# A hybrid decoder trunk on one core: matmuls of a stage grouped by width, attention distances seeded into the score banks by ScalarE, compress sums on 64 stationary columns

## The chip, the cores and the metric

The kernel runs on one core of a Trainium2 chip. The metric is the device time of one execution in microseconds. The core has TensorE (matmuls, with a weight load before each), VectorE, ScalarE, GpSimd and SyncE, which issues the DMAs; each takes its own queue of instructions in order.

## What is computed

Two layers over 256 tokens of 2048 features, in fp32. Each layer projects the normalized input with one matrix (2048 x 5696), whose columns feed three groups of heads; their outputs go through `w_out`, then an MLP of width 8192, then a gated per-layer embedding.

```python
def hybrid_layer(h, p_i, ...):
    proj = rms_norm(h, norm_mix_pre) @ w_in
    o_a = nsa_mixer(nsa_q, nsa_kv, nsa_g, nsa_cmp_w, nsa_cmp_pe)   # 16 heads in 4 groups, 64 wide
    o_b = rglru_mixer(...)
    o_c = gla_mixer(...)
    h = h + rms_norm(concatenate([o_a, o_b, o_c]) @ w_out, norm_mix_post)
    u = rms_norm(h, norm_mlp_pre)
    h = h + rms_norm(jnp.square(jax.nn.relu(u @ w_up)) @ w_down, norm_mlp_post)
    return h + jax.nn.sigmoid(h @ w_ple_gate) * (p_i @ w_ple)

def nsa_mixer(...):                       # three branches per head
    # compressed: 15 windows of 32 tokens, each summed with a learned weight to one key and one value
    k_cmp, v_cmp = compress(kc, cmp_w[0], cmp_pe[0]), compress(vc, cmp_w[1], cmp_pe[1])
    s = q @ k_cmp - slope * d_cmp         # then a softmax over valid windows, times v_cmp
    # selected blocks and sliding window, both with their own keys and values:
    s = q @ k - slope * distance          # causal softmax, times v
    return g0 * o_cmp + g1 * o_sel + g2 * o_win
```

With 256 tokens there are four blocks to select from and 16 may be selected, so all causal keys take part in the second branch, and the window of 512 covers everything too.

## The kernel before

Weights stream from HBM in units of 128 x 1024 elements. `ensure` takes a unit from a list in a fixed order (`plan`): SyncE loads it into `raw`, ScalarE casts it to `hi` (a shortened fp32 that TensorE takes at full rate), and VectorE makes the remainder `lo`. There are eight `hi` and eight `lo` buffers, so ScalarE and VectorE work up to eight units ahead, and a cast waits until TensorE has read the old content of its buffer. A product of two numbers is then three: hi x hi, hi x lo and lo x hi.

Two kinds of stage use the units. `form_a` keeps the activations stationary and moves 512 (or 256, 320) weight columns, three matmuls for each 128 rows of the weights. `form_b` keeps 128 columns of weights stationary and moves the activations: one matmul of 512 columns for `hi` (the activations' hi and lo side by side) and one of 256 columns for `lo`. It goes through the unit bank by bank: for each of `nf` banks of PSUM, for each of `kpu` blocks of rows, first the 512-column matmul, then the 256-column one. In the wide form (MLP) `nf` is 4 and `kpu` 2, in the narrow form (projections) 2 and 4, so a unit has eight pairs either way. A wide stage has eight units (64 pairs), a narrow one four (32 pairs); a layer has 15 wide and 16 narrow ones.

Attention and the recurrences are Python generators in a background list. After each unit `pump` runs pieces of them, each up to its next `yield`, so that their instructions stand among the projections; the number that a `yield` gives is an estimated time in us. Dependencies and the final order on each engine are worked out by the scheduler of the tile framework, which may move an instruction ahead of its place in the program when its inputs and buffers are ready.

`compress` (L705) builds blocks of the key and value inputs on VectorE and sums them with full-fp32 matmuls, each of which the profile shows as two instructions. The key sums keep 64 weight columns stationary and move 32; the value sums keep 128 block columns stationary and move 64 weight columns. Keys and values are done in one piece each, with one `yield` between them. `nsa` (L756) then has one piece for the scores of compressed keys, and for each of 8 pairs of heads three score tiles `S` of 512 columns. Each begins with a matmul of `idr` (an identity) with `dr` (the distances), which writes the distances into the bank (L804, L811); the products of queries with keys are added by the matmuls behind it. VectorE takes the maximum, ScalarE the exponentials straight from the bank, TensorE transposes and multiplies with the values, on 64 stationary columns in each half of the bank. `S` uses two banks (`sc`) in turn.

Of the kernel before, what the change touches and what calls it, by code (L numbers as in the profile page):

```python
# [18 lines left out]
P = 128  # L19
# [17 lines left out]
RATE = 1.02  # L37

C_D, C_DC, C_SL, C_SLC, C_RV, C_GM, C_SM = 0, 256, 288, 352, 384, 386, 514
C_ID = C_END = 770  # L40


def consts():
    c = np.zeros((P, C_END + P), np.float32)
    p = np.arange(P)
    slope = np.exp2(np.float32(-8.0) * np.arange(1, NH + 1, dtype=np.float32) / np.float32(NH)).astype(np.float32)
    c[:, C_ID:C_ID + P] = np.eye(P)
    c[:, C_D:C_D + 128] = p[None, :] - p[:, None] - 128
    c[:, C_D + 128:C_D + 256] = np.where(p[None, :] <= p[:, None], p[None, :] - p[:, None], NEG)
    for hf in range(2):  # L50
        t = p + 128 * hf
        d = t[:, None] - (16 * np.arange(15)[None, :] + 31)
        c[:, C_DC + 16 * hf:C_DC + 16 * hf + 15] = np.where(d >= 0, -d, NEG)
        c[:, C_DC + 16 * hf + 15] = 2 * NEG
        c[:, C_RV + hf] = (t >= 31)
    for cc in range(2):
        for f in range(4):
            for hf in range(2):
                for x in range(2):
                    sl = slope[8 * cc + 2 * f + x]  # L60
                    c[:, C_SL + (cc * 4 + f) * 8 + hf * 4 + x * 2:C_SL + (cc * 4 + f) * 8 + hf * 4 + x * 2 + 2] = sl
                    c[:, C_SLC + cc * 16 + hf * 8 + f * 2 + x] = sl
    c[:, C_GM:C_GM + P] = (p[:, None] <= p[None, :]) & (p[:, None] // 64 == p[None, :] // 64)
    c[:, C_SM:C_SM + 256] = (np.arange(256) % 64 != 0)[None, :]
    return c, slope
# [33 lines left out]
class Trunk:  # L99
# [66 lines left out]
    def cst(self):  # L166
        nc = self.nc
        self.c = self.sb.tile([P, C_END], F32, name="cst")
        self.id_ = self.sb.tile([P, P], F32, name="ident")
        self.dma(self.id_, self.a["cst"][:, C_ID:C_ID + P])  # L170
        self.ident = self.id_
        self.mhalf = self.sb.tile([P, 8], F32, name="mhalf")
        nc.gpsimd.memset(self.mhalf, -0.5)

    def cst2(self):
        nc, c = self.nc, self.c
        self.dma(c, self.a["cst"][:, 0:C_END])
        self.idr = self.sb.tile([P, P], F32R, name="idr")
        nc.vector.tensor_copy(self.idr, self.ident)
        self.dr = self.sb.tile([P, 288], F32R, name="dr")  # L180
        nc.vector.tensor_copy(self.dr, c[:, C_D:C_D + 288])


    def ensure(self, i):
# [74 lines left out]
    def form_b(self, base, nu, ut, evac, w=256, which=None, dst=None):  # L259


        nf, kpu = w // 128, 1024 // w
        accs = [self.acc() for _ in range(nf)] if which is None else self.banks(which)
        self.ensure(base)
        for u in range(nu):
            self.ensure(base + u)
            hi, lo = self.loaded[base + u]
            for f in range(nf):
                o = accs[f]
                for k in range(kpu):  # L270
                    kt = kpu * u + k
                    sl = slice(k * w + f * 128, k * w + f * 128 + 128)
                    last = u == nu - 1 and k == kpu - 1
                    self.mm(o, hi[:, sl], ut.both(kt), u == 0 and k == 0, False)
                    self.mm(o[:, 0:T], lo[:, sl], ut.get(kt)[0], False, last)
            self.ensure(base + u + NBUF)
            self.pump(1.4)
        for b in range(nf // 2):
            t = self.t2() if dst is None else dst
            for f in range(2):  # L280
                o, s = accs[2 * b + f], t[:, f * 256:f * 256 + 256]
                self.nc.scalar.copy(s, o[:, T:2 * T])
                self.tt(s, o[:, 0:T], s, ALU.add)
            if evac:
                evac(b, t)
# [419 lines left out]
    def compress(self, kc, wk, cm):  # L705
# [24 lines left out]
        for lp in range(16):  # L730
            for gp in range(2):
                self.mm(b[gp * 64:gp * 64 + 64, 0:32], wkv[0][:, lp], bk[:, lp, gp].rearrange("p c n -> p (c n)"),
                        lp == 0, lp == 15)
        kch = self.st([P, 2, 2, 16], "kch", 1, F32R)
        kcl = self.st([P, 2, 2, 16], "kcl", 1, F32R)
        nc.gpsimd.memset(kcl.bitcast(F32), 0.0)
        for gp in range(2):
            sl, so = slice(gp * 64, gp * 64 + 64), slice(64 - gp * 64, 128 - gp * 64)
            pv = b[sl, 0:32].rearrange("p (c n) -> p c n", c=2)
            nc.scalar.copy(kch[sl, :, gp], pv)  # L740
            nc.vector.tensor_sub(kcl[0:64, :, gp], pv, kch[sl, :, gp].bitcast(F32))
            nc.scalar.copy(kch[so, :, gp], pv)
        yield 0.3
        b = self.tr()
        for lp in range(16):
            self.mm(b[:, 0:64], bv[lp // 8][:, lp % 8].rearrange("p c g n -> p (c g n)"), wkv[1][:, lp], lp == 0, lp == 15)
        vc = self.st([64, 4, 64], "vcmp", 1)
        for g in range(4):
            for x in range(2):
                nc.scalar.copy(vc[x * 32:x * 32 + 32, g], b[g * 32:g * 32 + 32, 0:64])  # L750
        cm["kh"], cm["kl"], cm["v"] = kch, kcl, vc
        if self.dbg:
            self.dbg("vc", [vc, kch, kcl])
        yield 0.8

    def nsa(self, c, qa, kh, kl, v, cm, mhi, mlo):  # L756
        nc = self.nc
        qs = lambda j, hf: qa[j // 4][:, j % 4, hf * 128:hf * 128 + 128]

        S = self.sc()[:, 0:256]  # L760
        for hf in range(2):
            self.mm(S[:, hf * 128:hf * 128 + 128], self.idr,
                    self.dr[:, None, 256 + 16 * hf:272 + 16 * hf].to_broadcast([P, 8, 16]), hf == 0, False)
            for j in range(8):
                o = S[:, hf * 128 + j * 16:hf * 128 + j * 16 + 16]
                self.mm(o, qs(j, hf), cm["kh"][:, c, j // 4], False, False)
                self.mm(o, qs(j, hf), cm["kl"][:, c, j // 4], False, True)
        Sg = S.rearrange("p (x n) -> p x n", n=16)
        mx = self.sm(16)
        nc.vector.tensor_reduce(mx, Sg, axis=AX.X, op=ALU.max, negate=True)  # L770
        pc = self.t2().rearrange("p (x n) -> p x n", n=32)
        nc.gpsimd.memset(pc, 0.0)
        t = self.t2()[:, 0:256].rearrange("p (x n) -> p x n", n=16)
        self.tt(t, Sg, mx[:, :, None].to_broadcast([P, 16, 16]), ALU.add)
        self.tt(t, t, self.c[:, C_SLC + c * 16:C_SLC + c * 16 + 16, None].to_broadcast([P, 16, 16]))
        pcv = pc[:, :, 0:16]
# [6 lines left out]
                self.gtv[:, :, 8 * c:8 * c + 8])  # L783
        self.tt(pcv, pcv, den[:, :, None].to_broadcast([P, 16, 16]))
        pct = self.unit()
        pctv = pct.rearrange("p (j t) -> p j t", j=4)
        for jj in range(2):
            b = self.tr()
# [7 lines left out]
        for j in range(4):  # L796
# [4 lines left out]
            for st in range(3):  # L801
                S = self.sc()
                if st == 0:
                    self.mm(S, self.idr, self.dr[:, None, 128:256].to_broadcast([P, 4, 128]), True, False)  # L804
                    for x in range(2):
                        o = S[:, x * 256:x * 256 + 256]
                        self.mm(o, qs(2 * j + x, 0), kh[c][:, gp, :, 0:128], False, False)
                        self.mm(o, qs(2 * j + x, 0), kl[c][:, gp, :, 0:128], False, True)
                    m0, mw = 0, 4
                else:  # L810
                    self.mm(S, self.idr, self.dr[:, None, 0:256].to_broadcast([P, 2, 256]), True, False)  # L811
                    x = st - 1
                    self.mm(S, qs(2 * j + x, 1), kh[c][:, gp].rearrange("p b k -> p (b k)"), False, False)
                    self.mm(S, qs(2 * j + x, 1), kl[c][:, gp].rearrange("p b k -> p (b k)"), False, True)
                    m0, mw = 4 + 2 * x, 2
                nc.vector.tensor_reduce(mx[:, m0:m0 + mw], S.rearrange("p (x k) -> p x k", x=mw), axis=AX.X, op=ALU.max,
                                        negate=True)
                self.tt(nb[:, m0:m0 + mw], mx[:, m0:m0 + mw], sl8[:, m0:m0 + mw])
                pe = self.t2()
                kk = 512 // mw  # L820
                for x in range(mw):
                    h = 8 * c + 2 * j + (x // 2 if st == 0 else st - 1)
                    self.actf(pe[:, x * kk:x * kk + kk], S[:, x * kk:x * kk + kk], AF.Exp,
                              bias=nb[:, m0 + x:m0 + x + 1], scale=float(self.slope[h]),
                              accum_out=den[:, m0 + x:m0 + x + 1])
                pts.append((pe, m0, mw, kk))
                yield 1.1
# [21 lines left out]
            o = self.tr()[:, 0:T]  # L849
            g = 2 * c + gp  # L850
            for x in range(2):
                self.mm(o[x * 64:x * 64 + 64], cm["v"][x * 32:x * 32 + 16, g], pctv[x * 32:x * 32 + 16, j], True, False)
            for br in range(2):
                for kb in range(2):
                    for x in range(2):
# [247 lines left out]
```

## Time and profile before

| | |
|---|---|
| median of 3 runs | 2561.22 us (2560.81 to 2566.4) |
| the profiled execution | 2562.55 us, span 2560.8 us |
| TensorE busy | 2514.0 us, 98% of the span, 13062 matmuls |
| VectorE, ScalarE, GpSimd busy | 1533.5, 1258.8, 31.0 us |
| mean granted TensorE clock | 0.989 of full speed |

PE is TensorE's matmuls, PEld its weight loads, DVE VectorE, ACT ScalarE, POOL GpSimd. A matmul's row shows out<-moving,stationary. Matmuls overlap, so the mean duration of one is longer than the distance from one start to the next, and the pace of a row of matmuls is read from starts or from whole stretches.

### The profile page before, as it was taken

How to read it: one execution, taken by the hardware profiler on the slowest of the kernel's cores; microseconds unless marked ns; L12 is line 12 of the kernel's file. 1: busy time of each engine (PE TensorE's matmuls, PEld its weight loads, DVE VectorE, ACT ScalarE, POOL GpSimd, SP SyncE). 2: the span in 40 equal slices, each digit the busy share in tenths (PEclk: the TensorE clock that was granted, in tenths of full speed). 3: DMA queues.
4: the chain of work that ended last, by engine and by line, in shares of the span. 5: the costliest groups of instructions: out<-in, count | busy, mean ns of one | idle time of the engine just before them, and what ended most of it. 6: DMA issues, size and time to landing. Idle time of an engine off the chain costs nothing.

```text
span 2560.8 us, 33875 instructions
## 1 busy us (share of the span) xinstructions
PE 2514.0 (98%) x13062; PEld 2115.4 (83%) x13062; DVE 1533.5 (60%) x2088; ACT 1258.8 (49%) x1950; POOL 31.0 (1%) x41
## 2 busy tenths in 40 slices
PE   7999999999999999999999999999999999999999
PEld 7888888788888888887888788887888888888877
DVE  5665667764555555656666656677645556555564
ACT  6564546554443443444455555555544434444452
POOL 1000000000000000000010000000000000000000
PEclk9899999999999999999998999999999999999999
DMA  8543446556655556565564434555566556555653
GB/s 254 163 127 116 137 158 209 156 177 205 189 188 195 186 190 193 186 209 181 181 191 147 124 117 127 175 196 167 187 194 186 191 193 187 191 189 189 206 175 129
DMA packets 286369, 452.15 MB, mean 177 GB/s; under 512 B 32984, under 2 KB 107744, under 8 KB 286208
## 3 DMA queue, kind: packets, MB, share of 16 engines
q1 hardware_dynamic: 286208, 450.00, 55.0%
q8 instruction: 102, 1.67, 0.3%
q14 instruction: 59, 0.48, 0.1%
HBM read 447.85 MB, written 2.10 MB: 176 GB/s over the span
## 4 chain that ended last, share of the span: by engine, by line
PE 92%; DVE 4%; ACT 1%; DMA 1%; issue 1%; POOL 0%; SPq 0%; POOLq 0%; DVEq 0%; ACTq 0%
PE acc L164 61%; PE sc L164 15%; PE tr L164 15%; DVE lo L146 1%; DVE u L149 1%; PE tr L840 1%; PE tr L306 1%; ACT t L161 1%; DVE h L152 0%; DMA raw<-in_w_in_dram 0%; ACT hi L145 0%; DMA t<-in_p_dram 0%; DMA raw<-in_w_up_dram 0%; POOL sm L296 0%; DVE u L152 0%
## 5 line engine op out<-in xcount | busy, mean ns | idle before, releaser
L146 DVE TENSOR_TENSOR lo<-raw,hi 128x1024 fp32r<-128x1024 f32 (+1 forms) x832 | 1008.6, 1213 | 786.5 <-ACT hi L145 783.0
L145 ACT CAST hi<-raw 128x1024 fp32r<-128x1024 f32 (+1 forms) x832 | 867.1, 1044 | 1010.1 <-PE acc L164 586.5
L164 PE MATMUL acc<-hi,u 128*128 128x512 f32 (+2 forms) x2944 | 906.3, 386 | 14.8 <-ACT u L624 10.2
L164 PE MATMUL acc<-u,hi 128*128 128x512 f32 x1920 | 687.6, 401 | 0.0
L164 PEld LDWEIGHTS acc<-hi,u 128*128 128x128 f32 x2944 | 551.6, 190 | 123.1 <-ACT u L624 11.2
L164 PE MATMUL acc<-lo,u 128*128 128x512 f32 (+2 forms) x1472 | 567.4, 386 | 1.2 <-DVE lo L146 1.2
L164 PE MATMUL acc<-u,lo 128*128 128x256 f32 x1920 | 541.7, 282 | 0.0
L164 PEld LDWEIGHTS acc<-u,hi 128*128 128x128 f32 x1920 | 363.4, 189 | 87.8 <-issue 1.3
L164 PEld LDWEIGHTS acc<-u,lo 128*128 128x128 f32 x1920 | 364.9, 190 | 1.2 <-issue 0.3
L164 PEld LDWEIGHTS acc<-lo,u 128*128 128x128 f32 x1472 | 279.6, 190 | 53.2 <-DVE lo L146 1.7
L164 PE MATMUL tr<-u,hi 128*128 128x512 f32 x512 | 186.6, 399 | 0.0
L164 PE MATMUL sc<-u,hi 128*128 128x512 f32 x512 | 186.3, 398 | 0.0
L164 PE MATMUL sc<-u,lo 128*128 128x256 f32 x512 | 143.6, 281 | 0.0
L164 PE MATMUL tr<-u,lo 128*128 128x256 f32 x512 | 143.6, 280 | 0.0
L164 PE MATMUL sc<-hi,u 128*128 128x512 f32 x384 | 119.3, 389 | 0.0
L164 PE MATMUL tr<-hi,u 128*128 128x512 f32 x384 | 119.2, 389 | 0.0
L164 PEld LDWEIGHTS tr<-u,hi 128*128 128x128 f32 x512 | 96.2, 188 | 24.2 <-issue 0.6
L164 PEld LDWEIGHTS sc<-u,hi 128*128 128x128 f32 x512 | 96.2, 188 | 23.6
L164 PEld LDWEIGHTS sc<-u,lo 128*128 128x128 f32 x512 | 96.7, 189 | 0.4
L164 PEld LDWEIGHTS tr<-u,lo 128*128 128x128 f32 x512 | 96.7, 189 | 0.0
L164 PEld LDWEIGHTS sc<-hi,u 128*128 128x128 f32 x384 | 72.1, 188 | 15.1
L164 PEld LDWEIGHTS tr<-hi,u 128*128 128x128 f32 x384 | 72.1, 188 | 14.9
(177 smaller groups left out, 1786.8 us busy)
## 6 DMA issues: line engine op xcount, KB each, us to landing
raw<-in_w_up_dram SPq DMA_DIRECT2D x256, 512.0 KB, 3.6
raw<-in_w_down_dram SPq DMA_DIRECT2D x256, 512.0 KB, 3.5
raw<-in_w_in_dram SPq DMA_DIRECT2D x168, 512.0 KB, 3.5
raw<-in_w_out_dram SPq DMA_DIRECT2D x64, 512.0 KB, 3.8
raw<-in_w_ple_gate_dram SPq DMA_DIRECT2D x64, 512.0 KB, 4.4
raw<-in_w_in_dram SPq DMA_DIRECT2D x16, 256.0 KB, 2.9
raw<-in_w_ple_dram SPq DMA_DIRECT2D x8, 512.0 KB, 3.4
h<-in_x_dram SPq DMA_DIRECT2D x8, 256.0 KB
```

What stands on the lines that cost most here:

```text
L145: self.nc.scalar.copy(hi, src)
L146: self.nc.vector.tensor_sub(lo, src, hi.bitcast(F32))
L149: self.nc.vector.tensor_tensor(out, a, b, op=op)
L161: self.nc.scalar.activation(out, a, f, **k)
L164: self.nc.tensor.matmul(out, l, r, start=start, stop=stop, skip_group_check=True)
L306: self.nc.tensor.transpose(b[:, k * 128:k * 128 + 128], src[:, k * 128:k * 128 + 128], self.ident)
L840: nc.tensor.transpose(b[:, x * 128:x * 128 + 128], pe[:, x * 128:x * 128 + 128], self.ident)
```

## The change

- `form_b`: within a unit all 512-column matmuls come first, then all 256-column ones.
- `nsa`: the distances of the 512-column score tiles are copied into the bank by ScalarE (`seed`), and the matmuls add to them. Two matmuls at the very start of the program write both `sc` banks once. For the compressed scores the distances are added by VectorE after the matmuls.
- Compressed scores: the two parts of a key stand side by side in `kc2`, so one matmul of 32 columns replaces two of 16.
- `compress`: the value sums keep 64 weight columns stationary and move 128 block columns, even and odd terms in two halves of the bank; the two halves are copied, added and turned by one more product with two stacked identities. Keys and values have a `yield` after each quarter.
- The compressed values are padded with zeros to 128 rows (`self.vc`), and so are the probabilities (a memset of the lower half of `pct`).

```diff
-            for f in range(nf):
-                o = accs[f]
-                for k in range(kpu):
...
-                    self.mm(o, hi[:, sl], ut.both(kt), u == 0 and k == 0, False)
-                    self.mm(o[:, 0:T], lo[:, sl], ut.get(kt)[0], False, last)
+            for x in range(2):
+                for f in range(nf):
+                    o = accs[f]
+                    for k in range(kpu):
...
+                        if x == 0:
+                            self.mm(o, hi[:, sl], ut.both(kt), u == 0 and k == 0, False)
+                        else:
+                            self.mm(o[:, 0:T], lo[:, sl], ut.get(kt)[0], False, last)
...
+        for _ in range(2):
+            self.mm(self.sc(), self.id_, self.id_[:, None, :].to_broadcast([P, 4, P]), True, True)
...
+            if lp % 4 == 3:
+                yield 0.8
...
-            nc.scalar.copy(kch[sl, :, gp], pv)
-            nc.vector.tensor_sub(kcl[0:64, :, gp], pv, kch[sl, :, gp].bitcast(F32))
-            nc.scalar.copy(kch[so, :, gp], pv)
-        yield 0.3
+            nc.scalar.copy(kc2[sl, :, gp, 0], pv)
+            nc.vector.tensor_sub(kc2[0:64, :, gp, 1], pv, kc2[sl, :, gp, 0].bitcast(F32))
+            nc.scalar.copy(kc2[so, :, gp, 0], pv)
...
-            self.mm(b[:, 0:64], bv[lp // 8][:, lp % 8].rearrange("p c g n -> p (c g n)"), wkv[1][:, lp], lp == 0, lp == 15)
-        vc = self.st([64, 4, 64], "vcmp", 1)
+            x = lp % 2
+            self.mm(b[x * 64:x * 64 + 64, 0:128], wkv[1][:, lp], bv[lp // 8][:, lp % 8].rearrange("p c g n -> p (c g n)"),
+                    lp < 2, lp >= 14)
+            if lp % 4 == 3:
+                yield 0.8
+        vt = self.t2()[:, 0:128]
+        nc.scalar.copy(vt, b[:, 0:128])
+        b = self.tr()
+        self.mm(b[:, 0:64], vt, self.c[:, C_II:C_II + 64], True, True)
...
+    def seed(self, S, d, n):
+        self.nc.scalar.copy(S.rearrange("p (x k) -> p x k", x=n), d[:, None, :].to_broadcast([P, n, 512 // n]))
...
-            self.mm(S[:, hf * 128:hf * 128 + 128], self.idr,
-                    self.dr[:, None, 256 + 16 * hf:272 + 16 * hf].to_broadcast([P, 8, 16]), hf == 0, False)
...
-                self.mm(o, qs(j, hf), cm["kh"][:, c, j // 4], False, False)
-                self.mm(o, qs(j, hf), cm["kl"][:, c, j // 4], False, True)
+                self.mm(o, qs(j, hf), cm["k"][:, c, j // 4].rearrange("p x n -> p (x n)"), hf == 0 and j == 0, True)
...
+        for hf in range(2):
+            self.tt(t[:, hf], Sv[:, hf, :, 0], dc[:, hf, None, :].to_broadcast([P, 8, 16]), ALU.add)
...
+        self.tt(t, t, Sx[:, :, 1], ALU.add)
...
+        nc.gpsimd.memset(pct[64:128], 0.0)
...
-                    self.mm(S, self.idr, self.dr[:, None, 128:256].to_broadcast([P, 4, 128]), True, False)
+                    self.seed(S, self.c[:, C_D + 128:C_D + 256], 4)
...
-                    self.mm(S, self.idr, self.dr[:, None, 0:256].to_broadcast([P, 2, 256]), True, False)
+                    self.seed(S, self.c[:, C_D:C_D + 256], 2)
...
-                self.mm(o[x * 64:x * 64 + 64], cm["v"][x * 32:x * 32 + 16, g], pctv[x * 32:x * 32 + 16, j], True, False)
+                self.mm(o[x * 64:x * 64 + 64], self.vc[:, g, x], pctv[:, j], True, False)
```

## Rows read from the trace of the kernel before

**Rows 1.** The page, parts 1 (busy, share, instructions) and 4 (chain by engine).
```profile
PE 2514.0 (98%) x13062; PEld 2115.4 (83%) x13062; DVE 1533.5 (60%) x2088; ACT 1258.8 (49%) x1950; POOL 31.0 (1%) x41
...
PE 92%; DVE 4%; ACT 1%; DMA 1%; issue 1%; POOL 0%; SPq 0%; POOLq 0%; DVEq 0%; ACTq 0%
```

**Rows 2.** The chain in order of time: start us, us, what; a `form_b`, then a `form_a`.
```profile
675.19 22.61 PE acc L164 x128
...
743.03 21.79 PE sc L164 x96
```

**Rows 3.** Timeline of TensorE, a 256-column `form_a`: start, us, engine, line, out<-in, count.
```profile
1301.60 0.40 PE L164 MATMUL acc<-hi,u 128*128 128x256 f32 x2
1301.84 0.28 PE L164 MATMUL acc<-lo,u 128*128 128x256 f32 x1
1301.96 0.40 PE L164 MATMUL acc<-hi,u 128*128 128x256 f32 x2
```

**Rows 4.** Groups of TensorE by form: count, busy us, mean ns.
```profile
L164 PE MATMUL sc<-dr,idr 128*128 128x512 f32 x48 | 20.0, 417 | 0.0
...
L164 PE MATMUL sc<-kcl,u 128*128 128x16 f32 x64 | 15.8, 269 | 0.0
```

**Rows 5.** Timeline, a score tile of 512 columns.
```profile
230.44 0.39 PE L164 MATMUL sc<-dr,idr 128*128 128x512 f32 x1
...
230.67 0.63 PE L164 MATMUL sc<-u,u 128*128 128x256 f32 x4
```

**Rows 6.** Timeline of TensorE, compressed scores.
```profile
217.30 0.26 PE L164 MATMUL sc<-kch,u 128*128 128x16 f32 x1
217.41 0.26 PE L164 MATMUL sc<-kcl,u 128*128 128x16 f32 x1
```

**Rows 7.** Windows behind score stretches: busy us (count) by engine, granted clock (PEclk), DMA.
```profile
141.70:145.00 3.30, 3.30 (x13) 2.81 (x12) 3.17 (x8) 0.70 (x2) 0.00 (x0) 0.51 0.09 13
...
220.10:226.90 6.80, 6.80 (x21) 5.64 (x21) 2.68 (x5) 1.36 (x2) 0.15 (x1) 0.50 0.01 2
...
1411.95:1416.00 4.05, 4.05 (x24) 3.56 (x25) 3.86 (x10) 1.81 (x3) 0.00 (x0) 1.00 0.00 0
```

**Rows 8.** Timeline of TensorE, `compress` in layer 1; brackets: idle before, releaser.
```profile
82.82 0.30 PE L164 MATMUL tr<-u,u 128*64 128x32 f32 x2
85.41 1.13 PE L164 MATMUL tr<-u,u 128*64 128x32 f32 x32 [2.29 <-DVE u L149]
87.40 8.94 PE L164 MATMUL tr<-u,u 128*64 128x32 f32 x62 [0.87 <-DVE u L149]
```

**Rows 9.** Windows of `compress` and of what follows, both layers.
```profile
82.82:96.10 13.28, 10.12 (x98) 9.84 (x97) 8.73 (x22) 4.35 (x12) 0.00 (x0) 0.65 0.41 120
96.10:100.40 4.30, 4.30 (x15) 3.72 (x15) 0.42 (x1) 2.44 (x10) 0.00 (x0) 0.50 0.00 0
1354.90:1367.97 13.07, 10.85 (x95) 10.66 (x96) 8.35 (x20) 3.92 (x12) 0.00 (x0) 0.57 0.42 122
1367.97:1370.30 2.33, 2.33 (x9) 1.94 (x9) 0.14 (x1) 2.17 (x10) 0.00 (x0) 0.50 0.00 0
```

**Rows 10.** Timeline of TensorE, probabilities times values.
```profile
161.11 0.28 PE L164 MATMUL acc<-u,lo 128*128 128x256 f32 x1
161.32 0.65 PE L164 MATMUL tr<-u,vcmp 16*64 16x256 f32 x4
161.90 1.52 PE L164 MATMUL tr<-u,u 128*64 128x256 f32 x16
163.35 0.50 PE L164 MATMUL sc<-dr,idr 128*128 128x512 f32 x1
```

**Rows 11.** Groups of ScalarE by form.
```profile
L145 ACT CAST hi<-raw 128x1024 fp32r<-128x1024 f32 x816 | 857.2, 1052 | 1005.7 <-PE acc L164 584.9 <-PE tr L164 248.6 <-PE sc L164 65.7
...
L845 ACT COPY u<-tr 128x512 f32<-128x512 f32 x16 | 9.4, 590 | 0.1
```

**Rows 12.** Window of the attention stretch in layer 1: PE, PEld, DVE, ACT, POOL, PEclk.
```profile
100.00:340.00 240.00, 239.16 (x1375) 197.75 (x1374) 152.99 (x286) 136.57 (x299) 2.09 (x4) 0.98 0.45 135
```

More of the change, by code (lines that the diff above doesn't have):

```diff
@@ L39 @@
 C_D, C_DC, C_SL, C_SLC, C_RV, C_GM, C_SM = 0, 256, 288, 352, 384, 386, 514
-C_ID = C_END = 770
+C_II = 770
+C_ID = C_END = 834
 def consts():
@@ L47, in consts @@
     c[:, C_ID:C_ID + P] = np.eye(P)
+    c[:, C_II:C_II + 64] = np.concatenate([np.eye(64), np.eye(64)])
     c[:, C_D:C_D + 128] = p[None, :] - p[:, None] - 128
@@ L177, in cst2 @@
         self.dma(c, self.a["cst"][:, 0:C_END])
[L178 to L181, printed above, removed]
+        self.vc = self.sb.tile([P, 4, 2, 64], F32, name="vcmp")
+        nc.gpsimd.memset(self.vc, 0.0)
     def ensure(self, i):
@@ L267, in form_b @@
             hi, lo = self.loaded[base + u]
-            for f in range(nf):
-                o = accs[f]
-                for k in range(kpu):
-                    kt = kpu * u + k
-                    sl = slice(k * w + f * 128, k * w + f * 128 + 128)
-                    last = u == nu - 1 and k == kpu - 1
-                    self.mm(o, hi[:, sl], ut.both(kt), u == 0 and k == 0, False)
-                    self.mm(o[:, 0:T], lo[:, sl], ut.get(kt)[0], False, last)
+            for x in range(2):
+                for f in range(nf):
+                    o = accs[f]
+                    for k in range(kpu):
+                        kt = kpu * u + k
+                        sl = slice(k * w + f * 128, k * w + f * 128 + 128)
+                        last = u == nu - 1 and k == kpu - 1
+                        if x == 0:
+                            self.mm(o, hi[:, sl], ut.both(kt), u == 0 and k == 0, False)
+                        else:
+                            self.mm(o[:, 0:T], lo[:, sl], ut.get(kt)[0], False, last)
             self.ensure(base + u + NBUF)
@@ L733, in compress @@
                         lp == 0, lp == 15)
-        kch = self.st([P, 2, 2, 16], "kch", 1, F32R)
-        kcl = self.st([P, 2, 2, 16], "kcl", 1, F32R)
-        nc.gpsimd.memset(kcl.bitcast(F32), 0.0)
+            if lp % 4 == 3:
+                yield 0.8
+        kc2 = self.st([P, 2, 2, 2, 16], "kc2", 1, F32R)
+        nc.gpsimd.memset(kc2.bitcast(F32), 0.0)
         for gp in range(2):
@@ L739, in compress @@
             pv = b[sl, 0:32].rearrange("p (c n) -> p c n", c=2)
[L740 to L743 removed]
+            nc.scalar.copy(kc2[sl, :, gp, 0], pv)
+            nc.vector.tensor_sub(kc2[0:64, :, gp, 1], pv, kc2[sl, :, gp, 0].bitcast(F32))
+            nc.scalar.copy(kc2[so, :, gp, 0], pv)
         b = self.tr()
         for lp in range(16):
[L746 to L747 removed]
+            x = lp % 2
[7 more added lines that the diff above has]
+        self.mm(b[:, 0:64], vt, self.c[:, C_II:C_II + 64], True, True)
         for g in range(4):
             for x in range(2):
[L750 to L753, printed above, removed]
+                nc.scalar.copy(self.vc[x * 32:x * 32 + 32, g, x], b[g * 32:g * 32 + 32, 0:64])
+        cm["k"] = kc2
         yield 0.8
+    def seed(self, S, d, n):
+        self.nc.scalar.copy(S.rearrange("p (x k) -> p x k", x=n), d[:, None, :].to_broadcast([P, n, 512 // n]))
     def nsa(self, c, qa, kh, kl, v, cm, mhi, mlo):
@@ L758, in nsa @@
         qs = lambda j, hf: qa[j // 4][:, j % 4, hf * 128:hf * 128 + 128]
-        S = self.sc()[:, 0:256]
+        S = self.sc()
+        Sv = S.rearrange("p (h j x n) -> p h j x n", h=2, j=8, x=2)
         for hf in range(2):
-            self.mm(S[:, hf * 128:hf * 128 + 128], self.idr,
-                    self.dr[:, None, 256 + 16 * hf:272 + 16 * hf].to_broadcast([P, 8, 16]), hf == 0, False)
             for j in range(8):
-                o = S[:, hf * 128 + j * 16:hf * 128 + j * 16 + 16]
-                self.mm(o, qs(j, hf), cm["kh"][:, c, j // 4], False, False)
-                self.mm(o, qs(j, hf), cm["kl"][:, c, j // 4], False, True)
-        Sg = S.rearrange("p (x n) -> p x n", n=16)
+                o = S[:, (hf * 8 + j) * 32:(hf * 8 + j) * 32 + 32]
+                self.mm(o, qs(j, hf), cm["k"][:, c, j // 4].rearrange("p x n -> p (x n)"), hf == 0 and j == 0, True)
+        dc = self.c[:, C_DC:C_DC + 32].rearrange("p (h n) -> p h n", h=2)
+        t = self.t2()[:, 0:256].rearrange("p (h j n) -> p h j n", h=2, j=8)
+        for hf in range(2):
+            self.tt(t[:, hf], Sv[:, hf, :, 0], dc[:, hf, None, :].to_broadcast([P, 8, 16]), ALU.add)
+        t = t.rearrange("p h j n -> p (h j) n")
+        Sx = S.rearrange("p (g x n) -> p g x n", g=16, x=2)
+        self.tt(t, t, Sx[:, :, 1], ALU.add)
+        Sg = t
         mx = self.sm(16)
```

1 line of the change is left out of this document (removed).

## Prediction

> **What bounds the kernel now.** I read the page first. TensorE is busy for 2514.0 us of a span of 2560.8, and the chain that ended last is TensorE for 92% [rows 1]. So a nanosecond taken out of TensorE's stream comes off the end, and work of the other engines counts only where TensorE waits for it. Next I read the chain in order of time, which gives the pace of long runs of equal matmuls [rows 2], then TensorE's timeline in the stages that the diff touches [rows 3, 5, 6, 8, 10], and last the same stretches as windows, because they show the granted clock beside the work [rows 7, 9]. The reader is to see three things there. A stationary-weight stage (`form_b`) runs slower than its matmuls do in rows of one width. Each score tile begins with a TensorE matmul that only writes distances. And the two stretches of `compress` stand on TensorE with nothing else between, partly at half clock.
>
> **Grouping in `form_b`.** One stage of the MLP is 128 matmuls in 22.61 us [rows 2]: 64 pairs of a 512-column and a 256-column one, 0.3533 us a pair. Where only 512-column matmuls follow each other, 96 take 21.79 us, 0.2270 each [rows 2]; where only 256-column ones do, three take 0.36 us, 0.120 each [rows 3]. Together 0.3470, so alternating costs about 6.3 ns a pair. The plan has per layer 15 such stages of 64 pairs and 16 narrow ones of 32, in both layers 2944 pairs. After the change 8 of one width follow 8 of the other in each unit, so one of eight changes of width is left: 2944 x 6.3 ns x 7/8 = 16.2 us. Nothing in the trace shows 512-column matmuls back to back with these very operands, so the bounds are 0 and 18.6; I take 16.2, since the single-width rows come from the same engine with the same weight loads. By contrast, the Trainium skill (TensorE: Matmul & The Clock Gate, section Back-to-back issue gap) gives a gap that hangs on a matmul's own columns alone, columns/2.4 + 2.5 ns, which makes a pair 325 ns in any order and the regrouping worth nothing; this trace's 353 and 347 agree with neither that level nor that independence, but it is a rival below. A side effect: the banks of a stage now end within 8 short matmuls (1.0 us) of each other, so the first one is ready 3 x 2 x (0.353 - 0.120) = 1.4 us later than today, and its evacuation with it. The `dn` stage behind four such stages reads what the last of them made only after six other units of `hid`, 6 x 6 x 0.227 = 8.2 us, which hides it; without that cover it would cost at most 1.4 us in 8 places.
>
> **Seeds.** 48 matmuls of 512 columns [rows 4], 0.23 us each from start to the next start [rows 5], leave TensorE: 11.0 us. Eight narrower ones for the compressed scores, each between 0.11 [rows 6] and 0.23, taken at 0.15, give 1.2. In their place ScalarE makes 48 copies of 128x512 into the bank, 0.59 us each by the nearest copy [rows 11], 28 us in all. In the first attention stretch ScalarE is busy 136.6 us of 240 [rows 12], so 14 more fit. But a wait is new: the score matmuls now stand behind ScalarE's seed, and everything queued on TensorE stands behind them. ScalarE takes its queue in order, and its neighbours there are casts of 1.05 us [rows 11]. If a seed is ready when TensorE comes, it costs 0; if it stands behind one whole cast, 1.05 + 0.59 = 1.64 us, 48 times, 79 us. Today the score tiles already depend on ScalarE (a bank comes free when the exponentials two tiles earlier have read it) and TensorE is idle only 0.84 us in that stretch [rows 12]; a seed needs only that freed bank, and can be made while TensorE still works on projections. I take 0.1 us each, -5.
>
> **Compressed scores.** 64 pairs of 16-column matmuls [rows 4] become 64 single ones of 32 columns. They pace at 0.11 us [rows 6] with 16 columns, far above what 16 columns need, so 32 should pace alike: 64 x 0.11 = 7.0 us gained (bounds 3.5 and 7.0). VectorE gets three small additions per half, off the chain.
>
> **The clock behind the scores.** The four score stretches are followed by the half clock (1.2 GHz) in three cases, 3.3 and twice 6.8 us long (of the two long ones one stands), and by the full clock in one [rows 7]. What runs at half rate loses half its time: 16.9/2 = 8.4 us. With the stretches half as long, some of this goes; I cannot say which, so bounds 0 and 8.4, taken 4.
>
> **Compress.** Today it takes 13.28 and 13.07 us of TensorE, and 4.30 and 2.33 us of projections behind it run at 0.50 [rows 9], which loses 3.3: together 29.7 us. In it (layer 1; a product shows as two instructions) TensorE waits 2.29 and 0.87 us for VectorE's blocks, does half of the key sums, 32 instructions, in about 1 us, and then at half clock the rest of the keys and all 32 instructions of the value sums in 8.94 us [rows 8]. After the change the keys at full clock take 2 x 1.0 = 2.0; the value sums, 128 columns on 64 stationary ones, resemble the probability-times-value matmuls, 16 instructions (by the code 8 of 256 columns and 8 of 128) in 163.35 - 161.90 = 1.45 us [rows 10], so 0.06 us per 128 columns, 32 x 0.06 = 1.9; the added transposing product 0.2; the first wait for VectorE stays, 2.6. The work is cut into eight pieces between projections, and each change to 64 stationary columns costs: 161.11 to 161.32 is 0.21 where the next start usually comes after 0.12 [rows 10, 3]. In and out about 0.19, nine times, 1.7. The Trainium skill (TensorEngine Tiling (Array Packing), section Key Properties) says that a change of tiling mode drains the engine, which speaks against cutting the sums up; the 0.09 us agrees with a short drain. Sum per layer 8.4, both 16.8, and half of the present clock loss, 1.7, since the wait for VectorE that precedes the loss is still there: 18.5. Gain 11.2. If the clock falls as now, the keys' second half, the values and the changes cost double, 12.3 per layer and 3.3 behind: a gain of 2. If the wait goes as well, 18. ScalarE's copy between value sums and the product adds a wait of about 0.6 us where no projection is at hand; a projection normally is.
>
> **The rest.** The compressed-value matmuls take all 128 rows instead of 16: four took 161.32 to 161.90, 0.58 us [rows 10], four of the same 256 columns with 128 rows a third of 1.45, 0.48: 0.1 x 16 = 1.6 at most, taken 0.8. The two products at the start run while TensorE waits for its first inputs, the casts and memsets moved lie on VectorE and GpSimd with slack: 0, and no more than 3 if the first transposes had to wait for them.
>
> **Sum.** 16.2 + 12.2 - 5 + 7.0 + 4 + 11.2 + 0.8 = 46.4 us. The profiled execution took 2562.55 us (span 2560.8), 1.3 above the median of 2561.22; 2562.55 - 46.4 = 2516.2, against the median 2515.
>
> **Rivals.** (1) Order of widths does not matter: the 6.3 ns belong to these operands. For it: no row shows the grouped order. Against: at 2.4 GHz 512 and 256 columns are 213 and 107 ns, so the pure rows carry 13 to 14 ns each whatever the width, and the alternating pair 33. 2562.55 - 46.4 + 16.2 - 1.3 = 2531. The rule of the Trainium skill named above (TensorE: Matmul & The Clock Gate, Back-to-back issue gap) would have it end here. (2) The clock falls as now: the wait for VectorE that comes ahead of the loss in both layers stays in place. Compress gains 2, the scores 0: 13 less, 2528. (3) Seeds stand behind casts: ScalarE's casts wait for TensorE to free a weight buffer, then take 1.05 us, and a seed behind one comes 1.64 us after that. At 1.64 each the kernel takes 2562 - 51 + 79 = 2590. It ends above today's time when the mean wait passes (46.4 + 5)/48 = 1.07 us. For it: ScalarE is 57% busy there. Against: TensorE hardly waits there for anything today, though its score tiles hang on ScalarE's exponentials already.
>
> **Chances and range.** The forecast 0.50 (its own range 2502 to 2527), rival 1 0.20 (2518 to 2542), rival 2 0.18 (2515 to 2540), rival 3 0.12, of which 0.08 slower and 0.04 about even. A measurement of this kernel can tell about 0.2%, 5 us, from no change. So faster 0.88, same 0.04, slower 0.08. The range 2498 to 2545 leaves out rival 3 and a little on either side.
>
> **What would show it.** The pair pace of `form_b` falls to 0.347 (64 pairs in about 22.3 us); no `dr,idr` group is left and ScalarE has 48 copies into `sc`; TensorE's idle time between 100 and 340 us stays below 3 us (right) or has many waits for ScalarE at `sc` (rival 3); the windows of compress and of the scores show 1.00 or 0.50; the compress sums stand in pieces among projections. I would be wrong if 512-column matmuls of `form_b` pace above 0.23, if the reordering opens idle time at the ends of stages, or if scores waiting for seeds fill more than 20 us.

## The result and the profile after

The changed kernel takes 2524.12 us (median of 4 runs, 2521.38 to 2525.9) against 2561.01 us for the kernel before (4 runs, 2558.27 to 2566.4): a ratio of 0.9852, 95% interval 0.9834 to 0.9871. It is 1.5% faster, 9 us above the 2515 predicted and inside the range. The spans of the two profiled executions are 2560.8 and 2522.8 us, 38.0 apart, and the working below goes by these.

The page of the kernel after, parts 1 and 4, against [rows 1]:
```profile
PE 2479.9 (98%) x12950; PEld 2095.8 (83%) x12950; DVE 1531.9 (61%) x2098; ACT 1277.1 (51%) x2000; POOL 35.4 (1%) x46
...
PE 93%; DVE 3%; ACT 1%; issue 1%; DMA 1%; POOL 0%; SPq 0%; POOLq 0%; DVEq 0%; ACTq 0%
```
TensorE still sets the end, and what left its stream came off the time. Now the parts one by one. The chain, a wide `form_b` stage, against [rows 2]:
```profile
657.61 22.35 PE acc L166 x128
```
The wide stage is 0.26 us shorter; the `form_a` takes 21.79 us, as before. The timeline of TensorE inside that stage:
```profile
660.24 2.00 PE L166 MATMUL acc<-u,hi 128*128 128x512 f32 x8
662.08 1.12 PE L166 MATMUL acc<-u,lo 128*128 128x256 f32 x8
663.04 2.00 PE L166 MATMUL acc<-u,hi 128*128 128x512 f32 x8
```
From start to start, eight 512-column matmuls take 1.84 us (0.230 each, where [rows 2] give 0.2270) and eight 256-column ones 0.96 (0.120). The group of ScalarE's copies into the score banks, and the compressed scores of one half on TensorE, with the matmul behind them:
```profile
L771 ACT COPY sc<-cst 128x512 f32<-128x512 f32 x48 | 28.7, 601 | 5.5 <-DVE t L151 5.1
```
```profile
208.90 1.96 PE L166 MATMUL sc<-kc,u 128*128 128x32 f32 x16
210.71 0.48 PE L166 MATMUL acc<-hi,u 128*128 128x512 f32 x1
```
Sixteen of 32 columns take 1.81 us, 0.113 each. No `dr,idr` is left. The first attention stretch as a window (columns as in [rows 12]), and behind it what followed the scores, against [rows 7]:
```profile
94.00:330.00 236.00, 235.27 (x1434) 196.30 (x1435) 163.27 (x314) 155.68 (x348) 3.04 (x5) 1.00 0.49 145
```
```profile
136.00:148.00 12.00, 11.90 (x75) 10.51 (x74) 9.36 (x23) 9.86 (x28) 0.00 (x0) 1.00 0.59 172
...
211.00:223.00 12.00, 12.00 (x60) 10.04 (x59) 8.54 (x18) 7.54 (x17) 0.64 (x2) 1.00 0.31 89
```
TensorE is idle 0.73 us in 236, and in the list of its waits for that stretch ScalarE does not occur: TensorE does not wait for seeds there. The half clock behind the scores is gone. The timeline of `compress` in layer 1, against [rows 8]:
```profile
81.72 2.00 PE L166 MATMUL acc<-u,hi 128*128 128x512 f32 x8
83.56 1.11 PE L166 MATMUL acc<-u,lo 128*128 128x256 f32 x8
84.60 0.30 PE L166 MATMUL tr<-u,u 128*64 128x32 f32 x2
88.73 0.65 PE L166 MATMUL tr<-u,u 128*64 128x32 f32 x14 [3.83 <-DVE u L151]
89.31 3.61 PE L166 MATMUL acc<-u,hi 128*128 128x512 f32 x8
92.72 1.22 PE L166 MATMUL acc<-u,lo 128*128 128x256 f32 x8
93.87 1.12 PE L166 MATMUL tr<-u,u 128*64 128x32 f32 x32
...
112.50 2.00 PE L166 MATMUL acc<-u,hi 128*128 128x512 f32 x8
```
The same two projection matmuls that start the first and the last of these rows, in the kernel before:
```profile
79.95 0.39 PE L164 MATMUL acc<-u,hi 128*128 128x512 f32 x1
...
114.89 0.40 PE L164 MATMUL acc<-u,hi 128*128 128x512 f32 x1
```
From the one to the other it takes 30.78 us where it took 34.94, 4.2 less; the same pair in layer 2 takes 34.30 (1333.32 to 1367.62) where it took 37.16 (1351.61 to 1388.77), 2.9 less. The sums stand in pieces among projections, as forecast. But the wait for VectorE is longer (3.83 us, where it was 2.29 and 0.87; in layer 2 3.69, where it was 2.27), and the projection behind it takes 3.41 us for 1.84 at full rate. The windows of half clock in the kernel after (PEclk is the third column from the right):
```profile
24.00:29.00 5.00, 4.59 (x26) 4.59 (x27) 3.84 (x8) 2.64 (x6) 1.25 (x2) 0.66 1.04 165
89.00:93.00 4.00, 4.00 (x22) 3.18 (x19) 3.83 (x8) 0.04 (x1) 0.00 (x0) 0.57 0.44 131
451.00:459.00 8.00, 5.45 (x19) 4.50 (x20) 7.67 (x14) 4.08 (x9) 0.55 (x1) 0.57 0.23 68
1174.00:1179.00 5.00, 4.00 (x13) 3.29 (x14) 3.56 (x6) 3.06 (x8) 0.00 (x0) 0.66 0.38 111
1273.00:1281.00 8.00, 5.41 (x26) 5.41 (x27) 5.42 (x10) 2.14 (x6) 4.65 (x5) 0.57 1.14 209
1338.00:1346.00 8.00, 5.81 (x29) 4.97 (x30) 6.16 (x14) 1.00 (x2) 0.00 (x0) 0.57 0.36 103
1704.00:1711.00 7.00, 5.18 (x16) 4.17 (x17) 7.00 (x12) 3.98 (x8) 0.00 (x0) 0.51 0.19 67
2427.00:2432.00 5.00, 4.57 (x16) 3.65 (x16) 3.95 (x7) 2.86 (x7) 0.00 (x0) 0.66 0.39 128
```
and two places of the kernel before that answer to the third and fourth of them:
```profile
472.00:477.00 5.00, 4.99 (x20) 3.86 (x20) 5.00 (x10) 2.02 (x6) 0.00 (x0) 0.66 0.00 0
1192.00:1197.00 5.00, 3.55 (x18) 2.48 (x17) 4.78 (x9) 3.72 (x8) 0.00 (x0) 1.00 0.04 14
```
A window of length l at clock c loses l x (1 - c). Behind the scores 8.5 us of that went. But at the ends of the layers and at the start the clock now falls where it did not, or for longer: 8 x 0.43 = 3.4 us lost at 451 where it was 1.7 at 472, 1.7 at 1174 where it was none. Over the six of these windows that are not `compress` (all but 89 and 1338) it is 15.4 us, where the kernel before lost 1.7 at three places, 5.1. Idle time inside a window loses nothing, so this is an upper bound: followed matmul by matmul, the kernel after falls back at the six places by 1.5, 0.5, 1.6, 0.5, 0.7 and 1.6 us, 6.4 in all.

**Where the 38 us came from**, by the distances between starts on TensorE (waits taken out): seeds 13.6 us gone (48 large ones and 8 small), `form_b` in the MLP 678.0 to 671.2 (6.8), compressed scores 14.9 to 7.2 (7.8 before rounding), compressed values 1.5, clock behind the scores 8.5, of which 1.6 lies in those 7.8 already, compress 7.0 by the pairs above. In compress the sums went from 10.1 and 10.9 us to 4.75 and 5.15, but changes between 128 and 64 stationary columns were added and the waits grew by 2.1. Over all of `form_b` it is 1050.8 to 1042.7, 8.1; the 1.3 of it that lie in the projections are less half clock (5.2 us lost there before, 3.9 after). Together 43.6; less the 6.4 above 37.2, and 0.8 of the 38.0 are not assigned.

### The profile page after: what moved, and what is told of

It reads as the page before. It is cut to its first block, busy times and chain, and to the rows that moved or that the text cites. A ratio compares the mean times of both kernels' runs of the same rounds, so it can differ in the third digit from the quotient of the medians.

```text
span 2522.8 us, 33791 instructions
## 1 busy us (share of the span) xinstructions
PE 2479.9 (98%) x12950; PEld 2095.8 (83%) x12950; DVE 1531.9 (61%) x2098; ACT 1277.1 (51%) x2000; POOL 35.4 (1%) x46
## 4 chain that ended last, share of the span: by engine, by line
PE 93%; DVE 3%; ACT 1%; issue 1%; DMA 1%; POOL 0%; SPq 0%; POOLq 0%; DVEq 0%; ACTq 0%
PE acc L166 63%; PE tr L166 14%; PE sc L166 14%; PE tr L862 1%; DVE u L151 1%; DVE lo L148 1%; PE tr L311 1%; ACT t L163 1%; DVE h L154 0%; DMA raw<-in_w_in_dram 0%; DMA raw<-in_w_up_dram 0%; POOL sm L301 0%; DVE u L154 0%; DVE t L154 0%; DVE u L148 0%
## 5 line engine op out<-in xcount | busy, mean ns | idle before, releaser
L166 PE MATMUL acc<-u,hi 128*128 128x512 f32 x1920 | 494.2, 397 | 0.0
L166 PEld LDWEIGHTS acc<-u,hi 128*128 128x128 f32 x1920 | 347.0, 190 | 65.8 <-issue 2.7
L166 PEld LDWEIGHTS acc<-u,lo 128*128 128x128 f32 x1920 | 262.6, 191 | 18.9
L166 PE MATMUL acc<-u,lo 128*128 128x256 f32 x1920 | 268.9, 283 | 0.0
L166 PE MATMUL sc<-u,hi 128*128 128x512 f32 x512 | 140.3, 394 | 0.0
L166 PE MATMUL tr<-u,hi 128*128 128x512 f32 x512 | 138.4, 391 | 0.0
L147 ACT CAST u<-tr 128x256 fp32r<-128x256 f32 (+1 forms) x124 | 45.8, 379 | 80.8 <-PE tr L166 30.7
L166 PEld LDWEIGHTS sc<-u,lo 128*128 128x128 f32 x512 | 78.2, 189 | 10.0
L166 PEld LDWEIGHTS sc<-hi,u 128*128 128x128 f32 x384 | 72.1, 188 | 14.9
L166 PE MATMUL tr<-u,lo 128*128 128x256 f32 x512 | 82.9, 283 | 0.0
L166 PE MATMUL sc<-u,lo 128*128 128x256 f32 x512 | 81.3, 281 | 0.0
```

The source lines that it names most:

```text
L147: self.nc.scalar.copy(hi, src)
L166: self.nc.tensor.matmul(out, l, r, start=start, stop=stop, skip_group_check=True)
```

## The experiments

Each was timed in five rounds beside the kernel before (medians 2562.75, 2561.19 and 2561.34 us on the chips used). Unless another kernel is named, an edit is made to the kernel after. That kernel was not timed in the same rounds: differences to its 2524.12 are given below, and by the ratios to the kernel before they come out up to 2 us otherwise (key blocks first 12.3 less instead of 14.0).

| kernel | median us (lowest to highest) | ratio to before, 95% |
|---|---|---|
| form_b alternating again | 2528.76 (2526.04 to 2532.73) | 0.9868 [0.9854, 0.9883] |
| seeds by TensorE again | 2536.29 (2535.14 to 2537.77) | 0.9899 [0.9883, 0.9914] |
| before + grouping alone | 2554.83 (2552.82 to 2558.0) | 0.9972 [0.9962, 0.9983] |
| compress sums as before | 2533.75 (2532.6 to 2534.34) | 0.9886 [0.9873, 0.99] |
| key blocks first | 2510.12 (2507.2 to 2512.28) | 0.9804 [0.9785, 0.9822] |
| every second unit turned | 2522.28 (2521.1 to 2524.27) | 0.9849 [0.983, 0.9868] |
| seeds made twice | 2525.83 (2524.87 to 2527.43) | 0.9863 [0.9844, 0.9881] |
| compressed scores in halves | 2538.32 (2535.01 to 2540.32) | 0.9911 [0.9895, 0.9927] |
| key blocks first, units turned | 2509.53 (2509.06 to 2510.7) | 0.9799 [0.9786, 0.9812] |
| key blocks first, groups of two | 2510.84 (2509.86 to 2512.71) | 0.9804 [0.9791, 0.9818] |

**Form_b alternating again** (the inner loops of before in the kernel after).
```
-            for x in range(2):
-                for f in range(nf):
+            for f in range(nf):
...
-                        if x == 0:
-                            self.mm(o, hi[:, sl], ut.both(kt), ...)
-                        else:
-                            self.mm(o[:, 0:T], lo[:, sl], ut.get(kt)[0], False, last)
+                    self.mm(o, hi[:, sl], ut.both(kt), ...)
+                    self.mm(o[:, 0:T], lo[:, sl], ut.get(kt)[0], False, last)
```


> The changed kernel with form_b's old order, pairs of 512 and 256 columns alternating. Theory: a change of width costs, and grouping brings about 32 ns a unit (a wide stage 22.61 to 22.35 us in the two profiles, eight units), 368 units, so undoing it costs 12 us: 2536, with wide stages back at 22.6 us. The prediction's own term says 16 us: 2540. Rival (the order of widths does not matter, the stages got shorter through something else in the change): 2524, wide stages at 22.35.

It took 2528.76, 4.6 us more: less than either number expected, though not nothing. In its profile `form_b` is 8.2 longer. Two rows of its chain, two narrow stages and a wide one:
```profile
105.09 22.24 PE acc L166 x128
...
701.82 22.61 PE acc L166 x128
```
The wide one is back at [rows 2]. The narrow ones, also alternating, are as fast as pure rows (64 x 0.347 = 22.2). So alternating has two paces, and only one of them loses. What the time does not show of the 8.2 is mostly in `compress`:
```profile
85.45 0.65 PE L166 MATMUL tr<-u,u 128*64 128x32 f32 x14 [2.22 <-DVE u L151]
```
The wait is back from 3.83 to 2.22 us, and in layer 2 from 3.69 to 2.29. VectorE reads the first of the two banks of the projection ahead at 71.55 us here, and at 74.86 in the kernel after, right ahead of the second: with the widths grouped the banks end together, and the additions that make the blocks begin later.

**Before + grouping alone** (the same edit the other way, in the kernel before).
```
+            for x in range(2):
+                for f in range(nf):
...
```


> The kernel before with nothing but the grouped order in form_b. Theory: 12 us faster than before, 2549, with a wide stage at 22.35 us. The prediction's term: 16 us, 2545, a stage at 22.26. Rival: 2561. If it brings more than 16, the earlier freeing of the hi buffers counts too.

It took 2554.83, 8 us less than before where 12 or 16 were expected, and the wide stage of its chain is that of the kernel after; behind it the wait in its `compress`:
```profile
717.62 22.35 PE acc L164 x128
```
```profile
88.05 10.64 PE L164 MATMUL tr<-u,u 128*64 128x32 f32 x94 [3.94 <-DVE u L149]
```
Grouping is worth 8 us here and 4.6 in the kernel after, half of the term at most, and it alone lengthens the waits for VectorE (3.2 us in layer 1 before, 4.2 here). Going back to the chain of the kernel before, I found the row that I had passed over, and its timeline in the middle of that stage:
```profile
521.15 22.19 PE acc L164 x128
```
```profile
529.65 0.40 PE L164 MATMUL acc<-u,hi 128*128 128x512 f32 x1
529.88 0.28 PE L164 MATMUL acc<-u,lo 128*128 128x256 f32 x1
530.00 0.39 PE L164 MATMUL acc<-u,hi 128*128 128x512 f32 x1
530.23 0.27 PE L164 MATMUL acc<-u,lo 128*128 128x256 f32 x1
530.34 0.40 PE L164 MATMUL acc<-u,hi 128*128 128x512 f32 x1
```
Here two pairs take 530.34 - 529.65 = 0.69 us, 0.346 a pair: no loss, in the order said to lose 6.3 ns.

**Every second unit turned** (one change of width per unit instead of two).
```
-            for x in range(2):
+            for x in (0, 1) if u % 2 == 0 else (1, 0):
...
```


> The changed kernel with the two widths in alternating order from unit to unit (512, 256; 256, 512; ...), so that a stage changes its width half as often. Theory: in each unit the first five 512-column matmuls after the change are slow (about 20 ns in all above 227 each), and this goes in half of the 368 units: 3.7 us, 2520, with a wide stage at 22.27 us. Rival (the slow ones belong to the banks' order and not to the change of width): 2524, 22.35.

The stage took 22.27 us and the kernel 2522.28: 1.8 us below the kernel after, within the spread of the runs, so that the 3.7 expected are neither shown nor refuted; the stage is the one expected.

**Key blocks first, units turned** and **key blocks first, groups of two**, both on top of the experiment with the key blocks below (the first with the edit just shown); the second makes `form_b` two 512-column matmuls, then two 256-column ones, four times a unit.
```
+            order = [(f, k) for f in range(nf) for k in range(kpu)]
+            for p in range(0, 8, 2):
+                for x in range(2):
+                    for f, k in order[p:p + 2]:
...
```


> The key blocks first, as in the run before, and in every second weight unit the 256-column matmuls ahead of the 512-column ones, so that one change of width per unit is left instead of two. Theory (what a regrouped unit costs over a pure one hangs on the changes of width in it, about 10 ns each): wide stages at 22.27 us, and 368 units, one change less in each, 3 to 4 us less than with the key blocks alone: 2507 (2503 to 2511). Rival (what the turning of units saves is lost elsewhere): 2510 again. Both are far below the changed kernel's 2524; whether the two differ in the timed runs is open, since the spread of the runs is as large.

> The key blocks first, and form_b in groups of two: two 512-column matmuls, then two 256-column ones, four times per unit. If each change of width costs about 10 ns, as groups of eight and the turned units suggest, eight changes a unit instead of two make a unit 2.774 + 0.08 = 2.854 us, a wide stage 22.83, slower than strict alternation (22.61), and the kernel 368 x 0.06 = 22 us slower than with groups of eight: 2532. If short groups fall into a steady pace of their own, as strict alternation does (353 or 346.5 ns a pair), the stage lies between 22.2 and 22.6 and the kernel within 5 us of 2510. If the cost grows evenly from groups of eight to alternation, 22.5 and 2515.

They took 2509.53 and 2510.84, not to be told from the 2510.12 of the key blocks alone. The wide stage in groups of two:
```profile
698.79 22.29 PE acc L166 x128
```
Four times the changes of width, and no more time than groups of eight (22.35). That a change of width costs a fixed sum is refuted: the pace belongs to the sequence, as in strict alternation, and why is not shown.

**Seeds by TensorE again** (the constants laid out in another order to make room for `idr` and `dr`).
```
-                    self.seed(S, self.c[:, C_D + 128:C_D + 256], 4)
+                    self.mm(S, self.idr, self.dr[:, None, 128:256].to_broadcast([P, 4, 128]), True, False)
...
```


> The changed kernel with the 48 score tiles begun by TensorE's identity product again, all else as changed (the constants are laid out in another order to fit). Theory: ScalarE's seeds cost TensorE nothing, so undoing them costs the whole 48 x 0.23 = 11 us: 2535. Rival (the seeds make TensorE wait, and part of what they free is given back): 2524 to 2530. In the profile the seeds' products are back at 0.23 us each.

2536.29, 12.2 us more. The 48 matmuls take 12.1 us from start to start in its profile (10.6 us longer): the seeds' whole price, and no sign that ScalarE's seeds cost TensorE anything.

**Seeds made twice** (ScalarE copies each seed a second time, to the same place).
```
+        for _ in range(2):
+            self.nc.scalar.copy(S.rearrange(...), ...)
```


> The changed kernel in which ScalarE writes every seed twice, 48 more copies of 0.60 us. Theory: the seeds stand beside TensorE's work with slack, so 29 us more on ScalarE cost TensorE nothing: 2524 (up to 2526). Rival (TensorE already comes to the score tiles just as the seed is ready): 0.6 us for each tile, 2553.

The group of its copies:
```profile
L772 ACT COPY sc<-cst x96: 572/591/639, 134.1 to 1530.5; 128x512 f32<-128x512 f32 x96
```
48 more copies of 0.59 us on ScalarE, 28 us in all, leave the time 1.7 us higher (2525.83), within the spread of the runs. A seed is ready at least a copy's time before TensorE comes for it; the wait that I priced at 5, and the rival of seeds behind casts, have no footing.

**Compressed scores in halves** (each 32-column matmul as two of 16, as many as before the change).
```
+                for x in range(2):
+                    self.mm(o[:, 16 * x:16 * x + 16], qs(j, hf), cm["k"][:, c, j // 4, x], ...)
...
```


> The changed kernel with two 16-column matmuls for each of the 64 compressed scores instead of one of 32. Theory: the pace of these matmuls hangs on the weight load and not on the columns, 0.11 us either way, so 64 more cost 7 us; and with the stretches twice as long the half clock comes back behind some of them, up to 8.4 us more: 2531 to 2539. Rival (columns set the pace): 2524 to 2526.

2538.32, 14.2 us more. In the profile, 10.4 us longer, the scores take 13.8 us instead of 7.2. Its timeline, then its windows behind those scores:
```profile
211.97 3.74 PE L166 MATMUL sc<-kc,u 128*128 128x16 f32 x32
```
```profile
215.00:217.00 2.00, 2.00 (x11) 1.76 (x11) 1.19 (x4) 0.23 (x1) 0.67 (x2) 0.72 0.04 8
217.00:219.00 2.00, 2.00 (x6) 1.51 (x6) 0.99 (x3) 1.13 (x2) 0.00 (x0) 0.50 0.00 0
```
Twice the small matmuls, twice the time, and the half clock returns behind both score stretches of layer 1 (1.7 us each; not in layer 2, where the windows show 1.00). So the halved number gave the 7 us, and of the clock's 8.5 us the 3.4 that come back here; what keeps the clock up in layer 2 is not shown. The seeds are not the cause: with them back on TensorE (the experiment above) the granted clock is 1.00 over both attention stretches (100 to 340 and 1355 to 1600 us).

**Compress sums as before** (value sums with 128 stationary columns, one piece, no cuts).
```
-            self.mm(b[x * 64:x * 64 + 64, 0:128], wkv[1][:, lp], bv[...], lp < 2, lp >= 14)
+            self.mm(b[:, 0:64], bv[...], wkv[1][:, lp], lp == 0, lp == 15)
...
```


> The changed kernel with compress's sums as before: keys in one piece, values with 128 stationary columns in one piece, no turning product; the padded tile of values and the joined keys stay. Theory: of the 11 us forecast for this part only about 5 came, since TensorE still waits for VectorE's blocks (3.8 us in each layer) and the clock still falls to half behind that wait; undoing costs 5 us, 2529. Rival: the part is worth what was forecast and something else lost time, 2535; second rival: cutting it up cost as much as it gained, 2524. The clock of the stretch after the sums will read 0.50 for 4 us in layer 1 as before the change.

2533.75, 9.6 us more. Timeline and windows:
```profile
88.00 10.64 PE L166 MATMUL tr<-u,u 128*64 128x32 f32 x94 [3.94 <-DVE u L151]
```
```profile
88.00:98.60 10.60, 10.60 (x95) 10.54 (x96) 5.26 (x13) 1.83 (x7) 0.00 (x0) 0.50 0.37 100
98.60:103.60 5.00, 5.00 (x19) 4.18 (x19) 0.84 (x2) 4.71 (x14) 0.00 (x0) 0.59 0.00 0
```
In one piece all sums stand behind one wait, run at 0.50, and the low clock goes on behind them. In pieces, only the projection behind the first sums meets it. My theory for this run had the part at half its worth, and fell.

**Key blocks first** (VectorE builds all key blocks before any value block; the kernel after makes them in turn).
```
-        for l in range(2):
-            for gp in range(2):
-                for kv in range(2):
-                    for y in range(2):
+        for kv in range(2):
+            for y in range(2):
+                for l in range(2):
+                    for gp in range(2):
+                        blocks(kv, y, l, gp)
+                yield 1.3
```


> The changed kernel, in which VectorE builds all blocks of the keys before those of the values (the same 16 additions in another order). Theory: what the new compress still loses is TensorE's wait for the blocks, 3.8 us in each layer, and the half clock behind it, 3 to 5 us at half rate, so 1.5 to 2.5 lost. Eight additions of 0.56 us less stand ahead of the first key sum; the wait goes or is below 1 us, the clock stays at 1.00, and 8 to 11 us are gained: 2514. Rival: the wait moves to the value sums, or VectorE is late by its other work, and the time stays at 2524.

2510.12, 14 us less than the kernel after. One window over the whole of `compress` in layer 1:
```profile
83.00:104.00 21.00, 21.00 (x190) 17.89 (x188) 17.38 (x36) 10.93 (x24) 0.00 (x0) 1.00 0.50 135
```
TensorE is busy throughout, at full clock. Two rows of its timeline, the projections ahead of the first sums and those behind the last product:
```profile
81.83 2.00 PE L166 MATMUL acc<-u,hi 128*128 128x512 f32 x8
...
104.03 2.09 PE L166 MATMUL acc<-u,hi 128*128 128x512 f32 x8
```
Between these starts stand six units of projections, 2.79 us each (22.35/8) and 16.8 together; the rest of the 22.2, 5.4 us, is what the sums and their changes of stationary columns take in a layer without a wait.

With the wait the half clock behind it went, 12.1 us in both layers by the starts; the other 5 of the profile's 17 came at the start and the layers' ends, where this execution shows less half clock. That is more than the 8 to 11 expected.

## Why the prediction was right, and which step was off

The sum was 46.4 us and the profile shows 38.0. The sign and the bound (TensorE's stream) held, and so did most of the mechanisms; the sizes did not all. That the total came so near is in part luck: terms that were too large, by 9 us in grouping and 4 each in clock and compress, stand against a wait of 5 that did not come and seeds, scores and values that gave 3 more.

- **Grouping, 16.2: the term that was mis-sized.** It measured 6.8 in the profiles at one clock (8.1 with the half clock that left the projections), and 8 and 4.6 when timed alone and undone. The failing step is "2944 pairs at 0.3533": one slow stage was taken for all. The chain showed a stage of 22.19 us, and stages of projections ran at 0.347 a pair too: a unit of eight pairs there took 2.77 us, and grouped it takes 2.79. So the projections, for which the term had 1024 x 6.3 ns x 7/8 = 5.6, gave nothing between the two profiles at one clock, and 2.4 and 3.0 in those of the two experiments with the order alone. The other part of the error is in what grouping gives: 22.35, not the 22.26 of the sum, since the first five 512-column matmuls behind a change of width take 0.228 to 0.236 us and only the last three 0.227. The prediction had named a pace above 0.23 as a sign of being wrong, and the mean of eight is 0.230.
- **The side effect of grouping, 0:** the later end of the first bank was priced for the `dn` stage alone, where it is hidden. It came out in compress: 1.4 us had been reckoned, and in the kernel after, grouped instead of alternating, TensorE waits 1.6 and 1.4 us longer for VectorE in the two layers.
- **Rival 1, order without effect:** refuted by the grouping alone, 0.9972 [0.9962, 0.9983]. The rule of the Trainium skill behind it (TensorE: Matmul & The Clock Gate, section Back-to-back issue gap; given there for single matmuls, not for a stream with a weight load before each) disagrees with the traces in level (0.230 us for 512 columns in a group, by the rule 0.216) and in that the order counts (22.19 to 22.61 us for the same matmuls).
- **Seeds, 12.2:** right; 13.6 by the starts, 12.2 when undone.
- **The wait for ScalarE, -5:** wrong in the safe direction, 0. Even twice the copies added only 1.7, within the spread of the runs. The argument that a seed needs only the freed bank was the right one; the -5 was caution without a row.
- **Compressed scores, 7.0:** right, 7.8: 32 columns do pace like 16 (0.113 us each).
- **Clock behind the scores, 4:** at its upper bound there, 8.5. Yet 6.4 came back as half clock elsewhere, which no step of mine looked for. The experiment with scores in halves shows the cause of 3.4 of the gain; that of the loss stays open.
- **Compress, 11.2:** 9.6 when undone, 7.0 between the profiles, where the longer wait that grouping brings is counted in. The pieces stand as forecast, and the sums with their changes take 5.4 us a layer (forecast 5.8). A change to 64 stationary columns costs 0.08 us (eight 256-column matmuls and the change take 84.60 - 83.56 = 1.04, without it 0.96), near the 0.09 that was taken for the drain of the Trainium skill (TensorEngine Tiling (Array Packing), section Key Properties); that it is a drain no run shows. But "the first wait for VectorE stays, 2.6" was too low: with the widths grouped the blocks come later, and TensorE waits 3.8. The key blocks first show that this wait and the clock behind it were worth another 12 us. In the case "if the clock falls as now" the sum is off: keys' second half, values and changes are 1.0 + 1.9 + 1.7 = 4.6, so 13.0 a layer instead of 12.3 and a gain of 0.4 instead of 2; nothing that came out hangs on it.
- **Rival 2, the clock falls as now:** right in part. In compress the half clock stayed, for a quarter of its former length in layer 1 and half in layer 2 (by the windows 4.00 x 0.43 = 1.7 us lost and 8.00 x 0.43 = 3.4, where it was 6.8 in each); behind the scores it went.
- **Padded values, 0.8:** 1.5. The start: the first products lie in the wait for the first inputs, as taken.

Against the sum, grouping fell short by 9, the clock by 3.5 (8.5 less the 1.6 counted with the scores and the 6.4 that came back, where 4 was taken) and compress by 4; the wait that did not come gave back 5.

## What to carry to other kernels

Before a pace is multiplied by a count, list it for every stage of the same kind: one stage that runs the same sequence faster says that the cost hangs on more than the sequence. On a TensorE-bound kernel, a seed that another engine writes into the bank in time is worth its whole matmul, and a wait on TensorE should be priced with the half clock behind it: removing the wait for the key blocks gave 12 us, nearly as much as the largest part of the change. And a reordering that ends several banks at once is to be followed to every reader of the first of them: here it lengthened a wait in another part of the kernel.

## What the runs showed that was not expected

- One and the same alternating order of 512 and 256 columns runs at 0.353 or 0.346 us a pair for a whole stage. In the kernel before, the stage at 521 us is at the fast pace in layer 1; the same code in layer 2 is at the slow one. What chooses is not known, and no run here tests it.
- Groups of eight, of two, and turned units end at 22.35, 22.29 and 22.27 us a stage; the number of changes of width does not order them.
- Half clock at the ends of the layers differs between kernels that are alike there. Behind the same wait of 1.24 us TensorE ran at 0.66 in the kernel after (1174 to 1179) and at 1.00 with the key blocks first:
```profile
1167.00:1172.00 5.00, 3.69 (x20) 2.87 (x21) 4.78 (x9) 4.03 (x10) 0.00 (x0) 1.00 0.22 52
```
Each such stretch moves the time by 0.5 to 1.6 us in the two profiles, so differences of that size between these kernels are not put down to an edit here.
